# A period's second scale product behind a down projection's first column tile, and the last group of activations scaled two tiles later

## The chip, the cores and the metric

One Trainium2 chip, of which the kernel uses one core. The metric is the device time of one execution in microseconds, the median of three runs. TensorE is called PE here, VectorE DVE, ScalarE ACT, GpSimd POOL and SyncE SP.

## What is computed

The reference is one residual block on an input of 512 tokens by 2048 features: a normalised input goes through a combined projection into a gated linear recurrence and a banded attention, both are projected back and added, and a gated feed-forward follows. The change is in the feed-forward:

```
h2 = rms_norm(x, g_ffn[l])
up = causal_dwconv(h2 @ w_up[l], conv_w[l], conv_b[l])
a, gate = jnp.split(up, 2, axis=-1)
x = x + (a * jax.nn.silu(gate)) @ w_down[l]
```

w_up has 2 x 5632 columns, w_down 5632 rows and 2048 columns; all is float32 at entry and exit.

## The kernel before

The kernel is one program of straight code, and PE sets its pace. The feed-forward has 44 column pairs (`NPAIR_FF`); a pair is 128 columns of a and the 128 columns of gate that belong to them. The first four (`N_LEAD`) are made in `lead`. Each of the pairs 4 to 43 is a **unit** (`up_unit`): a Strassen scheme with seven products instead of eight, each of 8 x 3 small matmuls (`mm3`: high by high, high by low, low by high, in 16 bits). The products read weight tiles that ACT (line 889) and DVE (line 890) split into a high and a low half in `split16`. Behind each unit but the first stand two **downs** (`down`), each a block of w_down with two column tiles of 12 matmuls; DVE adds each column tile to the result (line 1078). One unit with its two downs is a **period**. 88 downs are listed in `DOWNS`; `N_BESIDE` = 78 of them stand beside units, ten follow the last unit.

**The order of the preparation.** `plan_unit` appends to the list `todo`, for each unit, seven steps (`start`, which splits the tile a22, then a11, s1, a11 again after an addition, a12, a12 again, s3), and then one `down_split` for each of its downs. Each step puts one split tile into `ready`. A product or a down begins with `take(3)`:

```
while len(ready) < 1 + n_ahead and todo:
    todo.pop(0)()
return ready.pop(0)
```

so that four tiles are ready before one is taken. Counted from the first step of a unit j with two downs, the steps are 0 to 6 for the products, 7 and 8 for the two downs, and step 9 is the `start` of unit j + 1. Product p takes step p, and steps up to p + 3 have been written by then.

**The scale chain.** Before its first split a period needs its scales. `period_scales(j, ds)` loads the two raw w_down tiles of the period (`down_loads`), has ACT sum the absolute values of each row of the unit's four raw tiles and of the two w_down tiles (`abs_sums`, line 895), and calls `scales`: DVE takes maxima (line 770), ACT writes them on a diagonal, one for the unit and one for the downs (line 771, tile `dg`, a pool with one buffer), PE multiplies the diagonals by ones (line 773, the small product), and DVE makes the scale and its inverse from the result (lines 774 to 776). `start` calls `period_scales` where the unit's dictionary has no "s" yet. `period_scales` also makes the scaled filter taps (lines 930 and 932).

The raw w_down tiles come from the tag "raw" of the pool `wp`, which has three buffers (in the last ten downs every second pair takes "ur" buffers); a split tile has three buffers of each of two tags. The loads of w_down, w_up and the rest are issued by SP (line 876), the accumulating ones by POOL (line 881).

**The activations.** Four units make one group of activations. `m_scale(g)` runs `scales` once over the group and `m_split` splits each of its four tiles (lines 856 and 857). These calls wait in the list `later`, from which each product runs one at its end; behind the last unit (43) the loop over `steps` runs all that are left, at once, before the down that follows it in `steps`. Downs 72 to 79 read group 9, downs 80 to 87 group 10, the group of units 40 to 43.

Program order is the priority with which the framework's scheduler lays the instructions into each engine's queue; the queues themselves run strictly in order.

Of the kernel before, what the change touches and what calls it, by code (L numbers as in the profile page):

```python
# [18 lines left out]
T = 512  # L19
# [4 lines left out]
NPAIR_FF = 44  # L24
# [28 lines left out]
def block_kernel(ctx: ExitStack, tc: tile.TileContext, xT, wst, cols, bias_t, masks, yT):  # L53
# [76 lines left out]
    def mm3(ps, sh, sl, mh, ml, start, stop):  # L130
        PE.matmul(ps, lhsT=sh, rhs=mh, start=start, stop=False)  # L131
        PE.matmul(ps, lhsT=sh, rhs=ml, start=False, stop=False)  # L132
        PE.matmul(ps, lhsT=sl, rhs=mh, start=False, stop=stop)  # L133


    colt = cst.tile([P, NC], F32, name="colt")
# [623 lines left out]

    def scales(sets, bound):


        n = len(sets)
        t = sm_t()
        dg = dgp.tile([P, 2, P], BF16, tag="dg", name=nm("dg"))
        for i, r in enumerate(sets):
            V.tensor_reduce(out=t[:, i:i + 1], in_=r, axis=mybir.AxisListType.X, op=ALU.max)  # L770
            A.activation(dg[:, i], ident, AF.Copy, scale=t[:, i:i + 1])  # L771
        psm = c3(mx_t()[:, 0:2 * P], 2)
        PE.matmul(psm[:, 0:n], lhsT=on1b, rhs=dg[:, 0:n], start=True, stop=True)
        V.tensor_reduce(out=t[:, 2:2 + n], in_=psm[:, 0:n], axis=mybir.AxisListType.X, op=ALU.max)
        V.tensor_scalar(out=t[:, 4:4 + n], in0=t[:, 2:2 + n], scalar1=1.01 / bound, scalar2=1e-30, op0=ALU.mult, op1=ALU.add)
        V.reciprocal(out=t[:, 6:6 + n], in_=t[:, 4:4 + n])
        return [(t[:, 4 + i:5 + i], t[:, 6 + i:7 + i]) for i in range(n)]
# [115 lines left out]
    def abs_sums(r, tiles):  # L893
        for k, t in enumerate(tiles):
            A.activation(junk_t(), t, AF.Abs, accum_out=r[:, k:k + 1])  # L895
# [15 lines left out]
        new = ur_t if at_end >= 0 and at_end % 4 == 0 else raw_t  # L911
        return [load(new(), N_DOWN + 8 * g + c2) for g, c2 in ds]

    def period_scales(j, ds):

        r = sm_t()
        sets = []
        u = units.get(j)
        if u is not None:
            abs_sums(r[:, 0:4], [u[n] for n in ("s1", "a22", "a11", "a12")])  # L920
            sets.append(r[:, 0:4])
        if ds:
            raws = down_loads(ds)
            abs_sums(r[:, 4:8], raws)
            sets.append(r[:, 4:4 + len(ds)])
        sc = scales(sets, BND)
        dt = [(raw, *sc[-1]) for raw in raws] if ds else []
        if u is not None:
            h = cwp.tile([P, 1], F32, tag="uh", name=nm("uh"))
            V.tensor_tensor(out=h, in0=sc[0][0], in1=inv_h, op=ALU.mult)  # L930
            cw = cwp.tile([P, 2, 3], F32, tag="cw", name=nm("cw"))
            A.activation(cw, c3(colt[:, C_CW:C_CW + 3 * 88], 2)[:, :, 3 * j:3 * j + 3], AF.Copy, scale=h)
            u.update(s=sc[0][1], cw=cw, ds=dt)
        return dt

    def plan_unit(j, ds):
        u = units.setdefault(j, {})

        def whl(n):
            ready.append(split16(u[n], u["s"]))  # L940

        def start():
            if "s" not in u:
                period_scales(j, ds)
            whl("a22")

        def s2():
            V.tensor_tensor(out=u["a11"], in0=u["s1"], in1=u["a11"], op=ALU.add)  # L948
            whl("a11")

        def s4():
            V.tensor_tensor(out=u["a12"], in0=u["a11"], in1=u["a12"], op=ALU.add)
            whl("a12")
            if j + 1 < NPAIR_FF:
                unit_loads(j + 1)

        def s3():
            i = N_MIX + 16 + 4 * (j - N_LEAD)
            u["s3"] = load_sum(raw_t() if j == N_LEAD else spare, i, i + 2)
            whl("s3")  # L960

        todo.extend([start, lambda: whl("a11"), lambda: whl("s1"), s2, lambda: whl("a12"), s4, s3])
        todo.extend([lambda k=k: down_split(u["ds"][k]) for k in range(len(ds))])

    def down_split(d):
        raw, inv, s = d
# [2 lines left out]
    def plan_downs(ds):  # L969

        st = []

        def one(k):
            if k == 0:
                st.extend(period_scales(None, ds))
            down_split(st[k])
        todo.extend([lambda k=k: one(k) for k in range(len(ds))])

# [45 lines left out]
    def lead():  # L1024
        half = N_LEAD // 2
        n = 0
        for j in range(half):
            u = c3(ur_t(), 2)
            for e in range(2):
                ps = mm_t()  # L1030
                for h in range(2):
                    wh, wl = next_w()
                    for k in range(8):
                        cs = slice(k * P, (k + 1) * P)
                        kt = 8 * h + k
                        mm3(ps, wh[:, cs], wl[:, cs], hh[kt], hl_[kt], kt == 0, kt == KT - 1)
                        if n == 0 and k == 3:
                            finish_r2()
                    if n in (2, 4, 6):
                        t_prep(n // 2 - 1)  # L1040
                    n += 1
                evict_r2(ps, u[:, e])
            lead_taps(j, [u[:, 0], u[:, 1]], (ssa, rmask)[j])
        unit_loads(N_LEAD)
        pss = [mm_t() for _ in range(2 * half)]
        for i in range(8):
            wh, wl = next_w()
            for e, kt in enumerate((i, i + 8)):
                for c in range(2 * half):
                    cs = slice((4 * e + c) * P, (4 * e + c + 1) * P)  # L1050
                    mm3(pss[c], wh[:, cs], wl[:, cs], hh[kt], hl_[kt], i + e == 0, i + e == 8)
            if i in (1, 2, 4, 6, 7):
                t_prep((0, 3, 4, 0, 5, 0, 6, 7)[i])
            if i == 4:
                period_scales(N_LEAD, [])
        us = [evict_r2(ps, actp.tile([P, T], F32, tag="act", name=nm("u"))) for ps in pss]
        later.extend([lambda j=j: lead_taps(half + j, us[2 * j:2 * j + 2]) for j in range(half)])

    def down(g, c2):
        t, inv_w = take(3)  # L1060
        mg, parts = groups[g]
        inv = cwp.tile([P, 1], F32, tag="inv", name=nm("inv"))
        V.tensor_tensor(out=inv, in0=inv_w, in1=mg[:, 1:2], op=ALU.mult)
        for cc in range(2):
# [5 lines left out]
            for ps, ts_ in zip(pss, cuts):  # L1070
                for k in range(4):
                    cs = slice((cc * 4 + k) * P, (cc * 4 + k + 1) * P)
                    cl = slice(1024 + (cc * 4 + k) * P, 1024 + (cc * 4 + k + 1) * P)
                    m = parts[k]
                    mm3(ps[:, ts_], t[:, cs], t[:, cl], m[:, ts_], m[:, T + ts_.start:T + ts_.stop], k == 0, k == 3)
            eng = nc.gpsimd if c < KT - 3 else nc.sync
            for ps, ts_ in zip(pss, cuts):
                V.scalar_tensor_tensor(out=acc[c][:, ts_], in0=ps[:, ts_], scalar=inv, in1=acc[c][:, ts_], op0=ALU.mult, op1=ALU.add)  # L1078
# [22 lines left out]
    for st in steps:  # L1101
        if isinstance(st, tuple):
            down(*st)
            continue
        up_unit(st)
        if st == N_LEAD:
# [3 lines left out]
        elif st % 4 == 3:  # L1110
            g = st // 4
            later.append(lambda g=g: (m_scale(g), m_split(4 * g)))
            later.extend([lambda j=j: m_split(j) for j in range(4 * g + 1, 4 * g + 4)])
        if st == NPAIR_FF - 1:
            while later:
                later.pop(0)()


def _level_masks(np):
# [121 lines left out]
```

## Time and profile before

| | |
|---|---|
| median of three runs | 2281.39 us (2280.96 to 2282.54) |
| the profiled execution | 2279.07 us, of which the span from the first to the last instruction is 2277.3 us |
| PE busy | 2200.5 us (97% of the span), granted clock 0.996 |
| DVE busy | 1672.4 us (73%) |
| ACT busy | 1336.8 us (59%) |
| moved by DMA | 294.21 MB, mean 129 GB/s |

"Busy" is the time in which an engine executes something, added up over the whole span; "granted clock" is TensorE's clock as a share of full speed. An idle time is named by the instruction that ended it, after the arrow.

### The profile page before, as it was taken

The page shows a single profiled execution, that of the slowest core. Times are in us where ns is not written, and L with a number is a line of the kernel's source. Part 1 is how long each engine was busy: PE and PEld are TensorE (multiplying, and loading weights), DVE is VectorE, ACT ScalarE, POOL GpSimd, SP SyncE. Part 2 cuts the span into 40 slices and gives each one's busy share as a digit, 9 for nine tenths or more (in the row PEclk, how much of TensorE's full clock was granted, in tenths as well). Part 3 has the DMA queues.
Part 4 walks back from the last instruction along what each step waited for, and adds up shares of the span by engine and source line. Part 5 has one row for each costly group of instructions (what it writes and reads, how often), then busy time and mean ns, then how long its engine had stood idle before and what let it go on. Part 6 is the DMA issues. An engine that isn't in the chain of part 4 may idle for free.

```text
span 2277.3 us, 34675 instructions
## 1 busy us (share of the span) xinstructions
PE 2200.5 (97%) x13667; PEld 1694.6 (74%) x13667; DVE 1672.4 (73%) x2729; ACT 1336.8 (59%) x2119; POOL 271.3 (12%) x261
## 2 busy tenths in 40 slices
PE   9999999999999999998999999999999999999989
PEld 7888888788888888785667777776776777777654
DVE  7678658857658744787777777787877777778764
ACT  5455445545445424457676767776667776767661
POOL 5223123310001103100000000000000000000001
PEclk9999999999999999999999999999999999999999
DMA  6222222232222333445555565555555666655532
GB/s 211 88 70 75 84 93 65 77 99 84 86 91 93 125 117 101 129 140 131 166 158 164 161 162 162 158 157 153 148 164 158 167 167 167 158 156 160 149 91 83
DMA packets 82755, 294.21 MB, mean 129 GB/s; under 512 B 9568, under 2 KB 10208, under 8 KB 82592
## 3 DMA queue, kind: packets, MB, share of 16 engines
q1 hardware_dynamic: 68112, 240.34, 32.4%
q0 software_dynamic: 14480, 51.65, 12.0%
q8 instruction: 107, 1.75, 0.3%
q14 instruction: 56, 0.46, 0.1%
HBM read 287.76 MB, written 4.19 MB: 128 GB/s over the span
## 4 chain that ended last, share of the span: by engine, by line
PE 49%; DVE 28%; ACT 11%; issue 6%; DMA 6%; POOL 0%; SPq 0%; ACTq 0%; DVEq 0%; POOLq 0%
PE mm L131 12%; PE mm L133 12%; PE mm L132 12%; DVE whl L890 8%; DMA raw<-wst 5%; ACT junk L895 4%; ACT whl L889 4%; DVE vo L1078 3%; PE mx L133 3%; PE mx L131 3%; PE mx L132 3%; DVE vo L828 2%; DVE vo L829 2%; DVE ur L948 1%; ACT dg L771 1%
## 5 line engine op out<-in xcount | busy, mean ns | idle before, releaser
L131 PE MATMUL mm<-th,whl 128*128 128x256 f16 x2240 | 612.5, 273 | 5.9 <-ACT whl L889 5.9
L133 PE MATMUL mm<-th,whl 128*128 128x256 f16 x2240 | 612.3, 273 | 2.6 <-DVE whl L890 2.6
L132 PE MATMUL mm<-tl,whl 128*128 128x256 f16 x2240 | 612.3, 273 | 0.0
L131 PE MATMUL mm<-act,whi 128*128 128x512 f32 x1024 | 406.4, 397 | 0.0
L133 PE MATMUL mm<-act,wlo 128*128 128x512 f32 x1024 | 399.4, 390 | 0.0
L131 PEld LDWEIGHTS <-whl 128*128 128x128 f16 x2948 | 289.1, 98 | 147.9 <-issue 32.0
L132 PE MATMUL mm<-act,whi 128*128 128x512 f32 x1024 | 398.8, 389 | 0.0
L133 PEld LDWEIGHTS <-whl 128*128 128x128 f16 x2948 | 289.2, 98 | 133.7 <-issue 22.5
L132 PEld LDWEIGHTS <-whl 128*128 128x128 f16 x2948 | 289.2, 98 | 108.5 <-issue 0.8
L889 ACT ACTIVATE whl<-ur,sm 128x1024 f16<-128x1024 f32 x206 | 231.1, 1142 | 154.2 <-DVE ur L948 52.1
L119 ACT CAST whi<-raw 128x1024 fp32r<-128x1024 f32 (+1 forms) x161 | 167.7, 1042 | 228.9 <-PE mm L132 183.7
L890 DVE SCALAR_TENSOR_TENSOR whl<-ur,sm,whl 128x1024 f16<-128x1024 f32 x206 | 261.4, 1277 | 41.0 <-ACT whl L889 41.0
L122 DVE TENSOR_TENSOR wlo<-raw,whi 128x1024 fp32r<-128x1024 f32 (+1 forms) x161 | 209.5, 1302 | 91.5 <-ACT whi L119 86.7
L131 PE MATMUL mx<-mhl,whl 128*128 128x512 f16 x708 | 268.5, 379 | 0.0
L132 PE MATMUL mx<-mhl,whl 128*128 128x512 f16 x708 | 268.4, 379 | 0.0
L133 PE MATMUL mx<-mhl,whl 128*128 128x512 f16 x708 | 268.2, 379 | 0.0
L133 PEld LDWEIGHTS mm<-act,wlo 128*128 128x128 f32 x1024 | 192.2, 188 | 41.2
L131 PEld LDWEIGHTS mm<-act,whi 128*128 128x128 f32 x1024 | 192.4, 188 | 38.8 <-issue 0.5
L132 PEld LDWEIGHTS mm<-act,whi 128*128 128x128 f32 x1024 | 192.5, 188 | 38.1 <-issue 0.5
L895 ACT ACTIVATE junk<-ur 128x1024 f16<-128x1024 f32 x146 | 152.1, 1044 | 0.0
L1078 DVE SCALAR_TENSOR_TENSOR vo<-mx,inv,vo 128x512 f32<-128x512 f32 x177 | 130.3, 741 | 25.1 <-PE mx L133 25.1
L890 DVE SCALAR_TENSOR_TENSOR whl<-raw,sm,whl 128x1024 f16<-128x1024 f32 x83 | 106.3, 1283 | 43.1 <-ACT whl L889 42.2
(285 smaller groups left out, 3022.7 us busy)
## 6 DMA issues: line engine op xcount, KB each, us to landing
raw<-wst SPq DMA_DIRECT2D x242, 512.0 KB, 3.5
ur<-wst SPq DMA_DIRECT2D x146, 512.0 KB, 3.5
spare<-wst SPq DMA_DIRECT2D x59, 512.0 KB, 4.8
ur<-wst POOLq DMA_DIRECT2D x40, 512.0 KB, 5.6
spare<-wst POOLq DMA_DIRECT2D x39, 512.0 KB, 8.0
vo<-xT SPq DMA_DIRECT2D x16, 256.0 KB, 5.3
vo<-xT POOLq DMA_DIRECT2D x16, 256.0 KB, 3.1
yT<-vo POOLq DMA_DIRECT2D x13, 256.0 KB, 2.3
```

Source lines behind the costliest of these rows:

```text
L119: A.copy(out=hi[:, c], in_=raw[:, c])
L122: V.tensor_tensor(out=lo[:, c], in0=raw[:, c], in1=hi[:, c].bitcast(F32), op=ALU.subtract)
L131: PE.matmul(ps, lhsT=sh, rhs=mh, start=start, stop=False)
L132: PE.matmul(ps, lhsT=sh, rhs=ml, start=False, stop=False)
L133: PE.matmul(ps, lhsT=sl, rhs=mh, start=False, stop=stop)
L771: A.activation(dg[:, i], ident, AF.Copy, scale=t[:, i:i + 1])
L828: V.scalar_tensor_tensor(out=y[:, 1:], in0=u[:, :T - 1], scalar=cw[:, 1:2], in1=y[:, 1:], op0=ALU.mult, op1=ALU.add)
L829: V.scalar_tensor_tensor(out=y[:, 2:], in0=u[:, :T - 2], scalar=cw[:, 0:1], in1=y[:, 2:], op0=ALU.mult, op1=ALU.add)
L889: A.activation(t[:, 0:1024], x, AF.Copy, scale=s)
L890: V.scalar_tensor_tensor(out=t[:, 1024:], in0=x, scalar=s, in1=t[:, 0:1024], op0=ALU.mult, op1=ALU.subtract)
L895: A.activation(junk_t(), t, AF.Abs, accum_out=r[:, k:k + 1])
L1078: V.scalar_tensor_tensor(out=acc[c][:, ts_], in0=ps[:, ts_], scalar=inv, in1=acc[c][:, ts_], op0=ALU.mult, op1=ALU.add)
```

## The change

`period_scales` is cut in two: `period_sums(j, ds)` (the loads and the sums of absolute values) and `period_scales(state, after)` (`scales` and what follows). The last `down_split` step of a unit j (step 8), from unit 5 on, now also calls `period_sums` for unit j + 1 and keeps its result in `sums_of`. The first down of a pair takes `take(1)` instead of `take(3)`, and behind the matmuls of its first column tile it calls `period_scales` on the kept result, with the small product ordered behind the last of these matmuls on PE (`issue_after` adds that order). `start` is left as it is, but for the call in it being written with both halves. At the end, the calls in `later` are no longer run right behind unit 43: the first of them (`m_scale` and one `m_split`) follows the down with number 77, the others the down with number 78.

```
-    def scales(sets, bound):
+    def scales(sets, bound, after=None):
...
-        PE.matmul(psm[:, 0:n], lhsT=on1b, rhs=dg[:, 0:n], start=True, stop=True)
+        with tc.issue_after(after.ins) if after is not None else ExitStack():
+            PE.matmul(psm[:, 0:n], lhsT=on1b, rhs=dg[:, 0:n], start=True, stop=True)
...
-    def period_scales(j, ds):
+    def period_sums(j, ds):
 
         r = sm_t()
-        sets = []
         u = units.get(j)
         if u is not None:
             abs_sums(r[:, 0:4], [u[n] for n in ("s1", "a22", "a11", "a12")])
-            sets.append(r[:, 0:4])
-        if ds:
-            raws = down_loads(ds)
-            abs_sums(r[:, 4:8], raws)
-            sets.append(r[:, 4:4 + len(ds)])
-        sc = scales(sets, BND)
-        dt = [(raw, *sc[-1]) for raw in raws] if ds else []
+        raws = down_loads(ds) if ds else []
+        abs_sums(r[:, 4:8], raws)
+        return j, r, raws
+
+    def period_scales(state, after=None):
+
+        j, r, raws = state
+        u = units.get(j)
+        sets = ([r[:, 0:4]] if u is not None else []) + ([r[:, 4:4 + len(raws)]] if raws else [])
+        sc = scales(sets, BND, after)
+        dt = [(raw, *sc[-1]) for raw in raws]
...
         def start():
             if "s" not in u:
-                period_scales(j, ds)
+                period_scales(period_sums(j, ds))
             whl("a22")
...
-        todo.extend([lambda k=k: down_split(u["ds"][k]) for k in range(len(ds))])
+        for k in range(len(ds)):
+            todo.append(lambda k=k: down_split(u["ds"][k]))
+        if ds and j + 1 < NPAIR_FF:
+            def sums(f=todo.pop()):
+                f()
+                sums_of[j + 1] = period_sums(j + 1, DOWNS[2 * (j - N_LEAD):2 * (j - N_LEAD) + 2])
+            todo.append(sums)
...
     def down(g, c2):
-        t, inv_w = take(3)
+        i = DOWNS.index((g, c2))
+        first = i % 2 == 0 and i < N_BESIDE - 2
+        t, inv_w = take(1 if first else 3)
...
-                    mm3(ps[:, ts_], t[:, cs], t[:, cl], m[:, ts_], m[:, T + ts_.start:T + ts_.stop], k == 0, k == 3)
+                    last_mm = mm3(ps[:, ts_], t[:, cs], t[:, cl], m[:, ts_], m[:, T + ts_.start:T + ts_.stop], k == 0, k == 3)
+            if first and cc == 0:
+                j = N_LEAD + 2 + i // 2
+                period_scales(sums_of.pop(j), last_mm)
...
             down(*st)
+            if st in DOWNS[N_BESIDE - 1:N_BESIDE + 1] and later:
+                later.pop(0)()
+                while later and st == DOWNS[N_BESIDE]:
+                    later.pop(0)()
             continue
...
-        if st == NPAIR_FF - 1:
-            while later:
-                later.pop(0)()
```

Two calls that the diff also touches keep their place: `plan_downs` and `lead` call the two halves one inside the other, and `mm3` returns its last matmul.

## Rows read from the trace of the kernel before

**Rows 1.** The page's first part: busy time, share and instructions of each engine.
```profile
PE 2200.5 (97%) x13667; PEld 1694.6 (74%) x13667; DVE 1672.4 (73%) x2729; ACT 1336.8 (59%) x2119; POOL 271.3 (12%) x261
```

**Rows 2.** Waits of PE over the whole span: us in total, times, longest.
```profile
PE mx L773 <- ACT dg L771: 46.8, 34, 9.7
```

**Rows 3.** Waits of PE from 1063 to 2170 us.
```profile
PE mx L773 <- ACT dg L771: 35.2, 31, 2.0
```

**Rows 4.** Stages: length, PE, PEld, DVE, ACT, POOL busy, clock, DMA.
```profile
1511.50:1631.40 119.90, 115.81 (x870) 84.92 (x869) 94.08 (x142) 83.49 (x126) 6.99 (x8) 1.00 0.57 158
...
1030.00:1063.00 33.00, 23.60 (x168) 17.89 (x168) 22.89 (x39) 22.93 (x37) 0.87 (x1) 0.85 0.46 132
1063.00:2170.00 1107.00, 1071.75 (x8042) 786.08 (x8041) 870.22 (x1317) 772.56 (x1159) 65.56 (x75) 1.00 0.59 160
```

**Rows 5.** Timeline of PE, one period: start, us, what.
```profile
1543.75 0.38 PE L131 MATMUL mx<-mhl,whl 128*128 128x512 f16 x1
...
1554.11 0.27 PE L131 MATMUL mm<-th,whl 128*128 128x256 f16 x1
...
1570.64 0.27 PE L773 MATMUL mx<-dg,on1b 128*128 128x256 bf16 x1 [0.65 <-ACT dg L771]
...
1583.73 0.27 PE L131 MATMUL mm<-th,whl 128*128 128x256 f16 x1
```

**Rows 6.** Timeline of ACT, the same period.
```profile
1563.70 1.13 ACT L889 ACTIVATE whl<-raw,sm 128x1024 f16<-128x1024 f32 x1
...
1568.82 1.06 ACT L895 ACTIVATE junk<-raw 128x1024 f16<-128x1024 f32 x1 [0.87 <-DMA raw<-wst]
...
1569.87 0.72 ACT L771 ACTIVATE dg<-ident,sm 128x128 bf16<-128x128 f32 x2
1571.89 1.15 ACT L889 ACTIVATE whl<-ur,sm 128x1024 f16<-128x1024 f32 x1 [1.30 <-DVE inv L1063]
1572.95 0.29 ACT L932 ACTIVATE cw<-colt,uh 128x6 f32<-128x6 f32 x1
```

**Rows 7.** Timeline of DVE, the same period.
```profile
1564.87 1.28 DVE L890 SCALAR_TENSOR_TENSOR whl<-raw,sm,whl 128x1024 f16<-128x1024 f32 x1 [1.83 <-ACT whl L889]
...
1573.07 1.28 DVE L890 SCALAR_TENSOR_TENSOR whl<-ur,sm,whl 128x1024 f16<-128x1024 f32 x1 [1.17 <-ACT whl L889]
```

**Rows 8.** Timeline of SP's issues, the same period.
```profile
1563.06 3.44 SPq L876 DMA_DIRECT2D raw<-wst  x2
```

**Rows 9.** The tile raw from 1150 to 2100 us.
```profile
DMA to landing us min/median/max: 4.7/5.7/9.4
```

**Rows 10.** The tile raw from 2180 to 2230 us.
```profile
DMA to landing us min/median/max: 3.5/3.5/3.6
```

**Rows 11.** The instructions of line 895 in four periods: length, ACT busy.
```profile
1511.50:1631.40 119.90, 25.95 (x48) 1.00 0.57 158
```

**Rows 12.** Groups of ACT's instructions by shape: count, busy, mean ns.
```profile
L856 ACT ACTIVATE mhl<-m,mg 128x512 f16<-128x512 f32 x42 | 27.9, 714 | 5.3 <-DVE mg L850 5.3
```

**Rows 13.** Timeline of PE behind the last unit.
```profile
2198.83 0.27 PE L133 MATMUL mm<-th,whl 128*128 128x256 f16 x1
2208.77 0.27 PE L773 MATMUL mx<-dg,on1b 128*128 128x128 bf16 x1 [9.67 <-ACT dg L771]
2208.83 0.63 PE L131 MATMUL mx<-mhl,whl 128*128 128x512 f16 x1
2209.26 0.63 PE L132 MATMUL mx<-mhl,whl 128*128 128x512 f16 x1
```

**Rows 14.** Stage behind that wait, columns as in rows 4.
```profile
2208.80:2214.00 5.20, 5.20 (x15) 1.96 (x15) 3.62 (x10) 4.02 (x7) 0.00 (x0) 0.55 0.01 3
```

**Rows 15.** Timeline of ACT behind the last unit.
```profile
2190.13 1.14 ACT L889 ACTIVATE whl<-raw,sm 128x1024 f16<-128x1024 f32 x1
...
2209.98 2.56 ACT L856 ACTIVATE mhl<-m,mg 128x512 f16<-128x512 f32 x4 [1.25 <-DVE mg L850]
...
2217.93 2.17 ACT L889 ACTIVATE whl<-raw,sm 128x1024 f16<-128x1024 f32 x2
```

More of the change, by code (lines that the diff above doesn't have):

```diff
@@ L132, in mm3 @@
         PE.matmul(ps, lhsT=sh, rhs=ml, start=False, stop=False)
-        PE.matmul(ps, lhsT=sl, rhs=mh, start=False, stop=stop)
+        return PE.matmul(ps, lhsT=sl, rhs=mh, start=False, stop=stop)
     colt = cst.tile([P, NC], F32, name="colt")
@@ L962, in plan_unit @@
         todo.extend([start, lambda: whl("a11"), lambda: whl("s1"), s2, lambda: whl("a12"), s4, s3])
-        todo.extend([lambda k=k: down_split(u["ds"][k]) for k in range(len(ds))])
+        for k in range(len(ds)):
[5 more added lines that the diff above has]
+            todo.append(sums)
+    sums_of = {}
     def down_split(d):
@@ L974, in one @@
             if k == 0:
-                st.extend(period_scales(None, ds))
+                st.extend(period_scales(period_sums(None, ds)))
             down_split(st[k])
@@ L1054, in lead @@
             if i == 4:
-                period_scales(N_LEAD, [])
+                period_scales(period_sums(N_LEAD, []))
         us = [evict_r2(ps, actp.tile([P, T], F32, tag="act", name=nm("u"))) for ps in pss]
```

## The prediction

> **What bounds the kernel now.** I read the busy times first: PE works 97% of the span, DVE 73%, ACT 59% [rows 1], so a change pays where PE stands still, and costs where it makes PE stand still. Then PE's waits, over the whole span: 46.8 us in 34 waits of the small product (line 773) for the diagonal that ACT writes [rows 2]. They are of two kinds. Between 1063 and 2170 us, the steady part, there are 35.2 us in 31 waits, none over 2.0 us [rows 3], which is 35.2 / 38 = 0.93 us for each of the units 6 to 43 and their periods. One wait alone, behind the last unit, is 9.67 us long [rows 13]. Third, the stages: four periods last 119.90 us, of which PE is busy 115.81, so 28.95 us a period is PE's floor; ACT is busy 83.49, or 20.87 a period, and DVE 94.08, or 23.5 [rows 4]. Last, the timelines of one period, from PE's first product matmul at 1554.11 to the next at 1583.73 us [rows 5], for what the chain does inside it.
>
> There the last sum of ACT begins at 1568.82 and ends by 1569.87, where the diagonals begin; the small product starts at 1570.64, 0.65 us after PE could have run it; the split of a22 follows on ACT at 1571.89 and on DVE from 1573.07 to 1574.35 [rows 5 to 7]. So from the end of the last sum to a finished a22 the chain takes 4.48 us. PE needs a22 only at 1583.73, or 1583.08 without the 0.65 us of waiting. The chain itself is 8.7 us early. PE waits not for its result but because the small product stands too early in PE's in-order queue. To move that product back looks right.
>
> **What the change adds: the work of a period's scales, twice.** The count of steps decides it. Product 5 takes with three ahead and so writes step 8; there the new code runs `period_sums` for unit j + 1. Product 6 still takes with three ahead (the diff leaves it), so it writes step 9, the `start` of unit j + 1. At that point no "s" is there: `period_sums` has not set it, only `period_scales` does, and that is called later, in the first down. So `start` runs both halves anew: it loads the same two w_down tiles again, sums all six tiles again, and issues its own small product, with no order imposed. The first down, after product 6, then runs `period_scales` on the first set of sums, and overwrites the scales. This happens for units 6 to 43, 38 times. `take(1)` in the first down comes one take too late to prevent it. The wait that should go belongs to the chain that stays.
>
> Per period the second set costs:
> - ACT: line 895 fills 25.95 us in four periods with 24 sums, 6.49 a period [rows 11]; two diagonals 0.72 and the taps 0.29 [rows 6]; together 7.5. ACT comes to 28.4 us of PE's 28.95.
> - SP: two more loads of 512 KB each, into the three "raw" buffers.
> - PE: one more small product. The period of rows 5 holds, besides the downs (1543.75 to 1554.11, 10.36 us), 169 matmuls in 29.62 - 10.36 - 0.65 = 18.6 us, 0.11 each; 38 of them are 4 us. The ordered product finds its diagonal ready, since its sums are the first set, and I cost no wait for it; the cover is the first column tile, 12 matmuls of 0.22, 2.6 us, ahead of it, and without that cover it would wait like the present one, up to 2.0 us.
> - DVE: five small instructions, near 1 us; it has 28.95 - 23.5 = 5.4 us idle, so nothing; with no idle time left it would be 38 us.
>
> Two moves are free. `period_sums` is written one product earlier, but its loads stand behind full buffers on SP and go out when these come free, as now; nothing on POOL is passed. `take(1)` leaves the split of a11 to the second down, two takes before its use; if ACT had no such lead, a split of 1.15 us [rows 6] would be late.
>
> **Where it shows: the chain of `start` comes late.** Of the three raw buffers, two hold the first set until the next unit's steps 7 and 8. The second set must pass through the third, one tile after the other. That buffer comes free when the old w_down tile has been split, at 1564.87 + 1.28 = 1566.15 [rows 7], just where SP issues the second of its raw loads now (1563.06 + 3.44 less the issue) [rows 8]. A load then lands 4.7 to 9.4 us later, 5.7 in the median [rows 9], by 1571.9. ACT meanwhile: now its sums end at 1569.87; in the hole of 0.87 us [rows 6] goes one of the four repeated unit sums, the other three follow to 1573.1, and the first repeated w_down tile to 1574.1. Only then can the second load be issued. With L for its landing, and 1.05 us for its sum, a22 is ready at 1574.2 + L + 1.05 + 4.48 = 1579.7 + L, against 1583.08. For L the rows of this stretch give 4.7 as the least and 5.7 as median, for pairs of loads [rows 9]; behind the last unit, with the queue empty, 3.5 [rows 10]. The second load goes alone, but into a stretch with other traffic, so I take 4.7: a22 is 1.3 us late. With 5.7 it is 2.3, with 3.5 about 0.1.
>
> The Trainium skill has another figure: "DMA: Bandwidth & Descriptors", section "Anatomy of one DMA", fits a GpSimd-issued transfer as 2.0 us plus its bytes over 436 GB/s, by which 512 KB would land in an estimated 3.2 us. By that page L + 1579.7 = 1582.9, just in time, and three periods in four would not wait at all. The trace does not agree: 4.7 is the least it shows in this stretch.
>
> One period in four also holds the four `m_split` of a group, 4 x 0.71 = 2.9 us of ACT ahead of the sums [rows 12], and its diagonal; they push the chain by about 3 us more, since ACT then has no hole. So the mean stall is (3 x 1.3 + 4.3) / 4 = 2.05 us in place of 0.93: +1.1 a period, 38 times, **+43 us**. The bounds: L of 3.5 gives (3 x 0.1 + 3.1) / 4 = 0.85, -3 us; L of 5.7 gives 3.05, +81 us.
>
> **The first units.** From 1030 to 1063 us PE is busy 23.60 of 33.00 us, with ACT at 22.93 and the clock at 0.85 [rows 4]: here splits already come late. Two or three doubled chains of 7.5 us fall into it or right behind; between 0 and 22 us, of which I take **8**.
>
> **The end.** Now PE stops at 2198.83 and goes on at 2208.77, and the next matmuls start 0.43 us apart instead of 10.36 / 48 = 0.22 [rows 5, 13]: the granted clock of those 5.20 us is 0.55 [rows 14], near the lower level of 1.2 GHz, after 9.67 us of idleness. 5.2 x 0.45 = 2.3 us go there, 12.0 in all. After the change two downs of group 9, 10.36 us, stand ahead of the small product, and two more ahead of the first use of group 10. Their tiles are split (the last by ACT from 2190.13) [rows 15]. The activations are scaled from 2209.98 as now and split by 2213, before PE needs them at 2199 + 20.7 = 2219.7. What is late next are the w_down tiles of down 80 and 81, split by ACT from 2217.93 to 2220.1 [rows 15], with DVE a good 1 us behind: at worst 2 us late, at best moved forward into ACT's holes, as their sums now stand ahead of `m_scale` in program order. **-11 us**, between -9.5 and -12.
>
> **Sum** against the profiled execution: 2279.1 + 43 + 8 + 4 - 11 = 2323; the median of the runs stood 2.3 above it, so **2325 us**, 1.9% slower. With the short landing and no start-up cost it is 2281.4 - 3 + 4 - 11 = 2271; with the long one and 22 us of start-up 2281.4 + 81 + 22 + 4 - 9.5 = 2379.
>
> **The rivals.**
> - *The doubled chain stays hidden* (ends on the other side). The a22 split is 8.7 us early; the doubling may use that up and no more. It is decided by the order on ACT: if the first repeated w_down tile is summed when it lands (1571.9) and not behind the unit's tiles, or if L is below 4, `start` is in time, PE's waits stay at about 0.9 us, and the end alone counts: 2281.4 + 4 - 11 = 2274, with the last of the present waits gone as well some 35 less, 2240. For it: ACT idles 1107 - 772.56 = 334 us in the 37 periods of the steady part, 9.0 each [rows 4], more than the 7.5 added. Against it: the two loads in series, which no idle engine shortens.
> - *ACT becomes the bound.* 28.4 us of work leave 0.5 us for waits, and ACT waits 9.0 a period now. If, late as it is, a half of these stay, a period takes 32.9 us against 29.9: +3.0 x 38 = 114, less the end: 2281.4 + 114 + 4 - 11 + 8 = 2396. For it: ACT and DVE answer each other in a22, in the addition to a11 and in the taps. Against it: ACT's waits shrink when it runs late.
> - *The change does what it says*, the 35.2 us go and the end too: 2281.4 - 35 - 11 = 2235. It would need `start` to find its scales, which the order of steps excludes, or the chain of `start` to be on time and its product placed late enough.
>
> **How the numbers follow.** A change of under 0.2%, 4.6 us, cannot be told from none. Chances: the forecast, a22 late by 1 to 3 us, 0.50 (its own range 2290 to 2365); ACT the bound, 2365 to 2430, 0.22; the doubling hidden, 2255 to 2287, 0.21, of which 0.07 lies within 0.2%; as it says, 0.07. Faster is 0.14 + 0.07 = 0.21, the same 0.07, slower 0.72. The range leaves out the 0.07 and about half of the ACT case: 2258 to 2390.
>
> **What would show it.** Right: line 895 with 228 activations more, ACT's busy time up by 38 x 7.5 = 285 us, 76 more loads, 40 MB; line 773 with 38 more matmuls, of which the ordered ones do not wait; PE waiting each period either for a22 (lines 131 or 133 for whl) or at the unordered small product; the 9.67 us gone, and no clock below full behind the last unit. The step on L is wrong if the second repeated raw load lands in 3.5 us or is not issued behind the sum of the first. The whole is wrong if the counts of lines 895 and 773 do not rise.

## The result and the profile after

The changed kernel takes 2621.97 us, the median of four runs (2613.67 to 2627.08), against 2281.18 us of the kernel before on the same chip (four runs too, with the three of the table before among them): a ratio of 1.1493, 95% interval [1.1459, 1.1527]. It is 14.9% slower. The forecast was 2325 us with a range of 2258 to 2390: the sign is right, and the size is far off.

The page's first part, after (compare [rows 1]); the span is 2622.5 us against 2277.3:

```profile
PE 2281.1 (87%) x13705; PEld 1716.8 (65%) x13705; DVE 1718.9 (66%) x2957; ACT 1608.4 (61%) x2689; POOL 271.2 (10%) x261
```

PE's idle time went from 2277.3 - 2200.5 = 76.8 us to 2622.5 - 2281.1 = 341.4, by 264.6 us; PE's busy time grew by 80.6. Together these are the 345.2 us of the span. ACT has 272 us more work (forecast 285), and PE 38 matmuls more, as forecast. So the work is doubled as the prediction said. What it costs is another matter.

In the changed file the small product is line 774, the sums line 896, the splits lines 890 and 891. PE's waits over the whole span (compare [rows 2]):

```profile
PE mx L774 <- ACT dg L771: 310.5, 42, 10.5
...
PE mm L131 <- ACT whl L890: 7.2, 4, 4.2
...
PE mm L133 <- DVE whl L891: 2.5, 2, 1.6
```

and from 1063 to 2510 us alone (compare [rows 3]):

```profile
PE mx L774 <- ACT dg L771: 294.1, 37, 10.5
```

In the steady part it is 294.1 / 37 = 7.9 us at each wait, where it was 0.93 a period and the prediction said 2.05. Only the small product waits; the waits for split tiles, where the prediction priced the stall, are 9.7 us in the whole run, against 8.5 before. PE's timeline shows which of the two small products it is (compare [rows 5]):

```profile
1532.75 0.27 PE L133 MATMUL mm<-th,whl 128*128 128x256 f16 x1
1540.70 0.37 PE L774 MATMUL mx<-dg,on1b 128*128 128x256 bf16 x1 [7.67 <-ACT dg L771]
1540.86 0.63 PE L131 MATMUL mx<-mhl,whl 128*128 128x512 f16 x1
1541.29 0.63 PE L132 MATMUL mx<-mhl,whl 128*128 128x512 f16 x1
...
1544.78 0.27 PE L774 MATMUL mx<-dg,on1b 128*128 128x256 bf16 x1
```

The product without an order, that of `start`, now stands behind the unit's last matmul and ahead of both downs; in [rows 5] it stands ahead of the unit's last 24 matmuls (1570.64 us, with the first matmul of the downs at 1573.37). The ordered one, 12 matmuls on, waits for nothing. Behind the wait the downs' matmuls start 0.43 us apart and not 0.22. Windows over the wait, the two downs and the next unit (columns as in [rows 4]):

```profile
1533.10:1540.70 7.60, 0.00 (x1) 0.00 (x1) 4.50 (x10) 4.40 (x8) 0.00 (x0) 0.74 0.19 71
1540.70:1552.60 11.90, 11.90 (x50) 5.27 (x50) 9.14 (x19) 6.58 (x11) 0.87 (x1) 0.88 0.39 100
1552.60:1571.00 18.40, 18.40 (x170) 16.45 (x168) 10.02 (x12) 15.44 (x25) 1.74 (x2) 1.00 0.84 232
```

Behind the idle stretch the first matmuls take twice their time, as at 1.2 GHz, the lower of the two levels; the granted clock of the downs' window is 0.88 on the mean, and it is back at 1.00 in the unit. That is where most of the 80 us of PE's busy time come from: the downs' 700 matmuls of line 131 take 297.9 us in all, against 266.3, and the units' 2240 still take 612.7, against 612.5.

ACT's timeline ahead of that wait (compare [rows 6]): six sums, six more, and both repeated w_down tiles with a wait of their own.

```profile
1521.28 1.04 ACT L896 ACTIVATE junk<-ur 128x1024 f16<-128x1024 f32 x1
...
1527.60 1.06 ACT L896 ACTIVATE junk<-raw 128x1024 f16<-128x1024 f32 x1
...
1531.78 1.04 ACT L896 ACTIVATE junk<-ur 128x1024 f16<-128x1024 f32 x1
...
1534.06 1.06 ACT L896 ACTIVATE junk<-raw 128x1024 f16<-128x1024 f32 x1 [1.15 <-DMA raw<-wst]
...
1538.87 1.06 ACT L896 ACTIVATE junk<-raw 128x1024 f16<-128x1024 f32 x1 [1.96 <-DMA raw<-wst]
...
1540.24 0.40 ACT L771 ACTIVATE dg<-ident,sm 128x128 bf16<-128x128 f32 x1 [0.22 <-DVE sm L770]
...
1543.16 1.13 ACT L890 ACTIVATE whl<-ur,sm 128x1024 f16<-128x1024 f32 x1
1546.92 1.15 ACT L890 ACTIVATE whl<-ur,sm 128x1024 f16<-128x1024 f32 x1 [2.62 <-DVE sm L777]
```

Without the second set the diagonal could have been written at 1528.7; it is written at 1540.24. The last line shows a second thing: the split of a11, behind that of a22, waits 2.62 us for a reciprocal. It is that of the second, ordered chain, which has replaced the scales of the first.

### The profile page after: what moved, and what is told of

It reads as the page before. It is cut to its first block, busy times and chain, and to the rows that moved or that the text cites. A ratio compares the mean times of both kernels' runs of the same rounds, so it can differ in the third digit from the quotient of the medians.

```text
span 2622.5 us, 35767 instructions
## 1 busy us (share of the span) xinstructions
PE 2281.1 (87%) x13705; PEld 1716.8 (65%) x13705; DVE 1718.9 (66%) x2957; ACT 1608.4 (61%) x2689; POOL 271.2 (10%) x261
## 4 chain that ended last, share of the span: by engine, by line
PE 54%; ACT 15%; DMA 15%; DVE 12%; issue 4%; POOL 0%; SPq 0%; ACTq 0%; DVEq 0%; POOLq 0%
DMA raw<-wst 13%; PE mm L131 10%; PE mm L133 10%; PE mm L132 10%; ACT junk L896 9%; PE mx L131 6%; PE mx L132 6%; PE mx L133 6%; DVE whl L891 4%; ACT whl L890 3%; ACT mhl L857 1%; DMA spare<-wst 1%; DVE wlo L122 1%; PE mx L774 1%; DVE wk L216 1%
## 5 line engine op out<-in xcount | busy, mean ns | idle before, releaser
L131 PE MATMUL mm<-th,whl 128*128 128x256 f16 x2240 | 612.7, 274 | 7.2 <-ACT whl L890 7.2
L132 PE MATMUL mm<-tl,whl 128*128 128x256 f16 x2240 | 612.5, 273 | 0.0
L131 PEld LDWEIGHTS <-whl 128*128 128x128 f16 x2948 | 294.8, 100 | 451.2 <-issue 347.8
L133 PEld LDWEIGHTS <-whl 128*128 128x128 f16 x2948 | 295.2, 100 | 134.0 <-issue 35.3
L132 PEld LDWEIGHTS <-whl 128*128 128x128 f16 x2948 | 296.1, 100 | 121.8 <-issue 27.1
L131 PE MATMUL mx<-mhl,whl 128*128 128x512 f16 x708 | 300.1, 424 | 0.0
L774 PE MATMUL mx<-dg,on1b 128*128 128x256 bf16 (+1 forms) x95 | 29.5, 310 | 310.5 <-ACT dg L771 310.5
L132 PE MATMUL mx<-mhl,whl 128*128 128x512 f16 x708 | 297.0, 419 | 0.0
L133 PE MATMUL mx<-mhl,whl 128*128 128x512 f16 x708 | 293.9, 415 | 0.0
L896 ACT ACTIVATE junk<-ur 128x1024 f16<-128x1024 f32 x279 | 290.5, 1043 | 0.0
L896 ACT ACTIVATE junk<-raw 128x1024 f16<-128x1024 f32 x158 | 165.9, 1051 | 95.8 <-DMA raw<-wst 95.1
L133 PEld LDWEIGHTS mm<-act,wlo 128*128 128x128 f32 x1024 | 192.2, 188 | 41.2
```

The source lines that it names most:

```text
L133: return PE.matmul(ps, lhsT=sl, rhs=mh, start=False, stop=stop)
```

## The experiments

Each was compared with the kernel before on its own chip (medians of 2279 to 2283 us).

**Without the doubling.** `once`: the changed kernel, in which the last product of units 5 to 42 takes with two ahead, so that `start` comes after `period_scales`.

```diff
-    def product(ps, b):
-        t = take(3)
+    def product(ps, b, n=3):
+        t = take(n)
...
-        product(bank[2][:, H:], T3)
+        product(bank[2][:, H:], T3, 2 if N_LEAD < j < NPAIR_FF - 1 else 3)
```

> The changed kernel with take(2) in the last product of a unit, so that start comes after the first down and finds its scales: every sum and every small product once. Theory A (the work done twice makes start's diagonal 8 us late, and its small product, ahead of both downs in PE's queue, holds PE for it): the 38 waits of about 8 us go, with them those of before (35 us), and the end gains 11: about 2235 us. Rival B (the product ordered behind the first column tile, or the summing one product earlier, is itself what costs): stays above 2500 us.

Measured: 2345.56 us, ratio 1.027 [1.025, 1.0289]. Nothing is doubled, and still it is 2.7% slower. The expectation failed, and the time lies far below the rival's too. The place behind the first column tile is itself a bad one, or the look-ahead that was given up for it. PE's waits:

```profile
PE mx L774 <- ACT dg L771: 55.3, 40, 5.7
PE mm L133 <- DVE whl L891: 32.7, 56, 1.6
PE mm L131 <- ACT whl L890: 14.1, 10, 3.3
```

Against the kernel before, the waits at the small product grew by 8.5 us, those for split tiles by 38.3 (from 8.5 to 46.8), and PE's busy time by 26.5 (from 2200.5 to 2227.0).

`once_early` asks whether the look-ahead that `once` gave up is the cause.

```diff
                 period_scales(sums_of.pop(j), last_mm)
+                while len(ready) < 3 and todo:
+                    todo.pop(0)()
```

> The kernel 'once' (nothing doubled, the single small product ordered behind the first column tile of the first down), but the steps that take(1) and take(2) held back, the split of a22 among them, are written right behind the scales in the middle of the first down, instead of at the second down. If 'once' lost its 64 us because its look-ahead came down to two tiles and a22's split was written too late, this one recovers them: 2250 to 2285 us, and the matmuls' waits for whl (47 us in 'once') go below 15. If the place itself is too late, because VectorE's evictions and additions of the first column tile stand ahead of the scale chain, the waits for whl stay and it ends at 2320 to 2350 us.

Measured: 2349.46 us, ratio 1.0283 [1.0253, 1.0312]. The look-ahead is not it. What is left is the place. PE's small product and DVE's timeline in this kernel:

```profile
1535.44 0.27 PE L774 MATMUL mx<-dg,on1b 128*128 128x256 bf16 x1 [1.30 <-ACT dg L771]
...
1537.10 0.42 DVE L775 TENSOR_REDUCE sm<-mx 128x2 f32<-128x256 f32 x1
1537.43 0.74 DVE L830 SCALAR_TENSOR_TENSOR vo<-z,cw,vo 128x510 f32<-128x510 f32 x1
1538.09 0.74 DVE L829 SCALAR_TENSOR_TENSOR vo<-z,cw,vo 128x511 f32<-128x511 f32 x1
1538.75 0.16 DVE L776 TENSOR_SCALAR sm<-sm 128x2 f32<-128x2 f32 x1
1538.82 0.74 DVE L1097 SCALAR_TENSOR_TENSOR vo<-mx,inv,vo 128x512 f32<-128x512 f32 x1
1539.48 0.74 DVE L830 SCALAR_TENSOR_TENSOR vo<-z,cw,vo 128x510 f32<-128x510 f32 x1
1540.14 0.15 DVE L777 RECIPROCAL sm<-sm 128x2 f32<-128x2 f32 x1
```

During a down DVE's queue holds the conv taps of the unit just done (lines 829 and 830) and the downs' additions (line 1097), and they stand between the chain's three short steps. From the product to the scales it takes 1540.29 - 1535.44 = 4.85 us, and a22 is split only behind that. No run took these instructions out of DVE's queue; that they are what costs is read from this timeline and from `p6end` below.

**The end alone.** `tail`: the kernel before with nothing but the move of the end.

```diff
             down(*st)
+            if st in DOWNS[N_BESIDE - 1:N_BESIDE + 1] and later:
+                later.pop(0)()
+                while later and st == DOWNS[N_BESIDE]:
+                    later.pop(0)()
             continue
...
-        if st == NPAIR_FF - 1:
-            while later:
-                later.pop(0)()
```

> The kernel before with the move of the last group's scaling alone. Theory: 9.67 us of wait and 2.3 us of slow clock go, up to 2 us come back as a late split behind them: 2270 us, 0.5% faster. Rival: a split or a scale product of the last ten downs is late in its place, and the end gains under 6 us.

Measured: 2281.1 us, ratio 0.9993 [0.998, 1.0007]. The 11 us don't come. PE's small products behind the last unit (compare [rows 13]):

```profile
2209.84 0.27 PE L773 MATMUL mx<-dg,on1b 128*128 128x128 bf16 x1 [5.69 <-ACT dg L771]
2217.00 0.22 PE L773 MATMUL mx<-dg,on1b 128*128 128x128 bf16 x1
2224.78 0.22 PE L773 MATMUL mx<-dg,on1b 128*128 128x128 bf16 x1 [2.38 <-ACT dg L771]
```

The product of `m_scale` at 2217.00 waits no more. The product of the downs 80 and 81 now stands ahead of it and waits 5.69 us, that of the next two downs another 2.38. That is 8.1 us in place of 9.67. The end of the changed kernel is no better: behind 2516 us PE waits 14.5 us in three times, of which 6.4 belong to the last period.

**One set of sums fewer at a time.** `noreload` is the changed kernel, where the second set sums the tiles of the first again, without loading them again.

```diff
-    def period_sums(j, ds):
+    def period_sums(j, ds, raws=None):
...
-        raws = down_loads(ds) if ds else []
+        if raws is None:
+            raws = down_loads(ds) if ds else []
...
-                period_scales(period_sums(j, ds))
+                period_scales(period_sums(j, ds, sums_of[j][2] if j in sums_of else None))
```

> The changed kernel, but start sums the w_down tiles that the first call has loaded instead of loading them again; ACT still sums everything twice, 7.5 us a period more than before. Theory A: the two loads in series go from the chain; the diagonal is then late by ACT's extra work alone, near 3.5 us at the boundary between unit and downs, instead of 8: about 2370 us, 2340 to 2420. Rival C (ACT with 28.4 us of work a period is the bound, whatever is loaded): 2580 us or more. Rival D (the loads alone do it): below 2290.

Measured: 2519.87 us, ratio 1.1036 [1.1018, 1.1055], in none of the ranges expected. The loads in series are 2621.97 - 2519.87 = 102 us of the loss, not most of it; 239 remain without them. The small product still waits 192.2 us in 37 times between 1063 and 2400 us, 5.2 each, where 3.5 were expected.

`noresum` leaves out the second set of sums as well; only `scales` and what follows it are still done twice.

```diff
-                period_scales(period_sums(j, ds))
+                period_scales(sums_of[j] if j in sums_of else period_sums(j, ds))
```

> The changed kernel, in which start takes the sums of step 8 instead of summing and loading again; only the scale chain (two diagonals, small product, five small instructions of VectorE) is still done twice, and the end is as changed. Theory A, the doubled sums and the serial loads are the whole loss, and the unordered small product of start is late only because they are: the sums are then those of the kernel before and stand one product earlier in the order, so start's product waits 1 to 2 us a period as before; the small product's second execution costs 38 x 0.1 = 4 us and ACT 1.0 us a period. About 2285 us, 2275 to 2300. Theory B, a second chain with a product ordered behind the first column tile costs by itself (the scales overwritten, splits and scales waiting for each other): 2330 us or more, with new waits of the downs' matmuls for whl or of the ordered product.

Measured: 2408.57 us, ratio 1.0561 [1.0545, 1.0577]. The repeated sums are 111 us, but theory A falls: a second chain of some ten short instructions costs over 120.

`start_once` has the same sums, one product earlier, and no second chain:

```diff
-                period_scales(period_sums(j, ds))
+                period_scales(sums_of.pop(j) if j in sums_of else period_sums(j, ds))
...
-            if first and cc == 0:
-                j = N_LEAD + 2 + i // 2
-                period_scales(sums_of.pop(j), last_mm)
```

> The sums in step 8 as in the change, but start takes them over and issues the one small product itself, where it stood before; no scales in the first down; the end as changed; look-ahead of three but for the take(1). Theory F (once lost 62 us by the later place of the chain, behind the first column tile, with scales that come late for a22): 2275 to 2285 us, as before. Rival G (the summing one product earlier delays ACT's splits): 2310 or more.

Measured: 2280.13 us, ratio 1.0001 [0.9988, 1.0013]: to write the sums earlier, `take(1)` and the end together cost and give nothing. ACT's diagonals and splits around the chain in `start_once`:

```profile
1513.02 0.72 ACT L771 ACTIVATE dg<-ident,sm 128x128 bf16<-128x128 f32 x2
...
1515.02 1.15 ACT L890 ACTIVATE whl<-ur,sm 128x1024 f16<-128x1024 f32 x1 [1.28 <-DVE uh L934]
...
1516.27 2.17 ACT L890 ACTIVATE whl<-ur,sm 128x1024 f16<-128x1024 f32 x2
```

and in `noresum`:

```profile
1526.47 0.72 ACT L771 ACTIVATE dg<-ident,sm 128x128 bf16<-128x128 f32 x2
...
1527.55 0.69 ACT L771 ACTIVATE dg<-ident,sm 128x128 bf16<-128x128 f32 x2 [0.36 <-PE mx L774]
1528.41 1.15 ACT L890 ACTIVATE whl<-ur,sm 128x1024 f16<-128x1024 f32 x1 [0.17 <-DVE sm L777]
...
1537.69 1.13 ACT L890 ACTIVATE whl<-ur,sm 128x1024 f16<-128x1024 f32 x1
```

The split behind that of a22 comes 1.25 us after it in the one and 9.28 us after it in the other. The second chain writes new scales, and every split from a11 on reads those.

`nouse` is the test of this: `noresum`, with the second chain still computed in full and its results left unused.

```diff
-            u.update(s=sc[0][1], cw=cw, ds=dt)
+            if use:
+                u.update(s=sc[0][1], cw=cw, ds=dt)
...
-                period_scales(sums_of.pop(j), last_mm)
+                period_scales(sums_of.pop(j), last_mm, False)
```

> 'noresum' (sums once, scale chain twice, 2408.6 us), in which the second chain is computed in full, small product, reduction, reciprocal and taps, but its results are left unused: all splits of the unit and of the two downs read the scales of start. Theory A, the 128 us that the second chain costs over 'start_once' come from the splits that must wait for its scales: a11 and all behind it are split only when the reduction behind the first down's first column tile has passed VectorE's queue, so the w_down splits, the loads that wait for their buffers and the next period's last sum come late. Then this kernel gives nearly all back: 2280 to 2305 us. Theory B, the chain's own work and its places in the queues of ACT, VectorE and PE cost it: it stays at 2390 to 2410 us.

Measured: 2301.1 us, ratio 1.0099 [1.0079, 1.0118], within A's figures. 107 of the 128 us come from splits that wait for scales which were already there once; 21 are the chain's own work and places. The 107 us show on PE as shorter waits at the small product (58.2 us in 42 times, against 129.6 in 45 in `noresum`) and as 39.6 us less of busy time. The expectation's path from late splits over late loads to a late sum fits: ACT's sums wait 15.2 us for raw loads between 1100 and 2100 us, against 50.1 in `noresum`; no run tested that path by itself. `noreload_nouse` makes the same edit in `noreload`.

> 'noreload' (sums twice, chain twice, 2519.9 us) with the second chain's results left unused in the same way. If the repeated sums, 6.5 us of ACT ahead of start's product, cost their 111 us whatever the second chain does: 2281 + 111 = 2390, 2370 to 2410 us. If they cost only because the second chain has already made the period's splits late, and would be hidden in ACT's idle time without it: 2290 to 2340 us. If the second chain's overwriting costs nothing: 2520 again.

Measured: 2463.34 us, ratio 1.0818 [1.0792, 1.0844], between the ranges expected. The repeated sums are not hidden without the other loss. They cost 2463.34 - 2301.1 = 162 us by themselves and 111 beside it, so the two losses overlap in part, and no single figure belongs to either.

**The same doubling in the kernel before.** `dup_before` calls `period_scales` twice in `start` and is the kernel before otherwise.

```diff
                 period_scales(j, ds)
+                if j > N_LEAD + 1:
+                    period_scales(j, ds)
```

> The kernel before, with start computing each period's scales twice (loads, sums, small product), and nothing else of the change. Theory A (the doubled work, waited for at small products ahead of the downs, is the whole loss): 2560 to 2650 us, waits of 6 to 9 us a period at the small products. Rival E (the change's other parts, less look-ahead and the summing in step 8, carry a good part of it): below 2480.

Measured: 2532.34 us, ratio 1.1092 [1.1068, 1.1116], a little under the range expected. So doubling costs 250 us with nothing moved. In the change it is 341. The difference was not taken apart; in `dup_before` both chains run ahead of the first split, so no split waits for scales that are written anew in the downs, and no set is held across a unit.

**The order itself.** `nopin` takes only the order off the ordered product.

```diff
-                period_scales(sums_of.pop(j), last_mm)
+                period_scales(sums_of.pop(j))
```

> The changed kernel without the order on the second small product (no issue_after); the double work stays. Theory A: the ordered product never waited, so 2600 to 2640 us as the changed kernel. Rival B (the ordering holds PE or pushes start's product to its place): below 2500 us.

Measured: 2629.51 us, ratio 1.1517 [1.1493, 1.154], the changed kernel's time to within 0.3%. The order that gave the change its name does nothing for the time here, since the ordered product already stands behind that column tile by its place in the program: in `nopin` too it runs 12 matmuls behind the other.

`dup_late` meant to keep the doubling and move `start`'s product behind the first down.

```diff
-            if "s" not in u:
-                period_scales(period_sums(j, ds))
+            if "s" not in u or j > N_LEAD + 1:
+                period_scales(period_sums(j, ds), seen.get("mm"))
...
+            seen["mm"] = last_mm
             if first and cc == 0:
```

> The work stays doubled, but take(2) in a unit's last product moves start with its second small product behind the first down, so PE has 5.2 us of matmuls ahead of the place where it waits. Theory A (it is the place of the product in PE's queue that turns the late chain into a wait): the wait falls by about those 5 us a period; 2345 (the same kernel without the doubling) plus 0 to 100: 2345 to 2450 us. Rival C (ACT's work of 28.4 us a period is the bound wherever PE waits): 2550 us or more.

Measured: 2700.5 us, ratio 1.1836 [1.1814, 1.1858], far from theory A's range. It lies in rival C's, but ACT is busy 1598.3 us of 2698.5, 59%, so ACT's work is not the bound here. The later place in the program moved the repeated sums back in ACT's queue too, behind the taps, so the product's waits rose to 362.2 us in 42 instead of falling. The run does not separate the place of the product from that of its sums, and decides nothing on the place.

**A better place.** `p6end` is the kernel before, with the small product ordered behind the last matmul of the unit's seventh product; the step is written right there.

```diff
-        PE.matmul(psm[:, 0:n], lhsT=on1b, rhs=dg[:, 0:n], start=True, stop=True)
+        with tc.issue_after(pin[0].ins) if pin else ExitStack():
+            PE.matmul(psm[:, 0:n], lhsT=on1b, rhs=dg[:, 0:n], start=True, stop=True)
...
+        pin.append(mm)
+        while len(ready) < 3 and todo:
+            todo.pop(0)()
+        pin.clear()
...
-        product(bank[2][:, H:], T3)
+        product(bank[2][:, H:], T3, 2)
```

> The kernel before, with the small product of start ordered behind the last matmul of the unit's last product instead of ahead of its 24 matmuls (the step runs right behind these matmuls; sums, loads and look-ahead as before). Theory F (the chain is up to 2.0 us late at the old place, and 2.6 us of matmuls now stand ahead): the 35 us of steady waits go, a22 is still 6 us early: 2246 us, 1.5% faster. Rival: the later place delays the scales' chain on DVE, and PE waits for splits instead: 2275 or more.

Measured: 2251.76 us, ratio 0.9869 [0.9852, 0.9885]: 1.3% faster than before. The small product of this kernel and DVE's timeline:

```profile
1500.15 0.27 PE L776 MATMUL mx<-dg,on1b 128*128 128x256 bf16 x1 [0.46 <-ACT dg L773]
...
1500.46 0.42 DVE L777 TENSOR_REDUCE sm<-mx 128x2 f32<-128x256 f32 x1
1500.80 0.68 DVE L1013 TENSOR_TENSOR z<-mm,z 128x512 f32<-128x512 f32 x1
1501.40 0.16 DVE L778 TENSOR_SCALAR sm<-sm 128x2 f32<-128x2 f32 x1
1501.46 0.41 DVE L1014 TENSOR_TENSOR z<-mm,z 128x256 f32<-128x256 f32 x1
1501.80 0.15 DVE L779 RECIPROCAL sm<-sm 128x2 f32<-128x2 f32 x1
```

From the product to the scales it is 1501.95 - 1500.15 = 1.8 us, where it was 4.85 behind the first column tile: only two evictions of the unit stand between, and the taps begin later. Between 1063 and 2150 us PE waits at the small product 8.1 us in 18 times, against the 35.2 in 31 of [rows 3].

`p6end_tail` adds the end's move to it, as the diff of `tail` shows it.

> The kernel 'p6end' (small product ordered behind the last matmul of the unit's last product, 2251.8 us) with the change's move of the end added. If the move of the end is worth nothing, because the wait is handed to the next pair's small product, as in 'tail': 2250 us, 2248 to 2253. If it adds its 10 us: 2241.

Measured: 2250.81 us, ratio 0.9867 [0.9852, 0.9882]: nothing gained, as in `tail`. `best` orders the products of the last downs in the same way, each behind the last matmul of a down.

```diff
+        end = DOWNS.index((g, c2)) >= N_BESIDE - 2
-        t, inv_w = take(3)
+        t, inv_w = take(2 if end else 3)
...
+            if end and cc == 1:
+                pin.append(mm)
+                while len(ready) < 3 and todo:
+                    todo.pop(0)()
+                pin.clear()
```

> 'p6end' with the end moved, and the last pairs of downs treated as the units are: their small product ordered behind the last matmul of the down ahead of it. If the end's wait is a matter of place in PE's queue as the units' was, the 8.1 us that 'tail' still waited go: 2238 to 2245 us. If the diagonal of those pairs is late for another reason (their loads or ACT's queue), the wait moves to the next matmul, for whl: 2248 to 2253 us.

Measured: 2242.24 us, ratio 0.9827 [0.9812, 0.9842], the fastest of all, 1.7% under the kernel before. PE's waits over its whole span (compare [rows 2]):

```profile
PE mx L776 <- ACT dg L773: 13.3, 23, 2.2
```

Behind 2150 us these waits are 2.7 us in two times, against 9.5 in two in `p6end_tail`. So the end did have some 9 us to give (2250.81 - 2242.24), and they hung on the place of the last pairs' products in PE's queue, not on that of `m_scale` alone.

## Why the prediction was wrong

**The doubling: right.** `start` finds no scales and does the whole period again, 38 times: ACT +272 us against 285, 40 MB more, 76 raw loads more. Without it (`start_once`) the loss is gone.

**The chain's timing: nearly right.** The second repeated w_down tile goes alone behind the sum of the first. Forecast was a sum that ends 1574.2 + 4.7 + 1.05 us, with the unit's end at 1583.73 - 10.36 = 1573.4, so 6.6 us behind it; measured, the sum that begins at 1538.87 ends 6.9 us behind the unit's last matmul, which ends at 1533.0. The load is issued behind the sum of the first, as forecast, at 1535.23, and its landing was even shorter than the 4.7 us chosen: the second sum begins 1538.87 - 1535.12 = 3.75 us after the end of the first.

**The step that failed: the price of the lateness.** The prediction charged it at the first use of a22 in the next unit, two downs later: "a22 is 1.3 us late". Among the signs it did name a wait "at the unordered small product", but no term of its sum prices one. `start`'s small product stands ahead of both downs in PE's queue, which runs in order: no matmul and no weight load of the downs ran in the 7.67 us. The cover of 10.36 us, which the downs were to give, is behind the waiting instruction and covers nothing. Charged there, the prediction's own figures give a diagonal at 1574.2 + 4.7 + 1.05 = 1579.95 and the product 0.77 us on [rows 5, 6], at 1580.7, against 1573.4: a wait of 7.3 us, and the period shown has 7.67. (The place behind the unit's last matmul is read from the trace after; at the place of [rows 5], where PE could have run the product from 1569.99 on, the same diagonal gives 10.7.) In the steady part that is 38 x (7.3 - 0.93) = 242 us before the groups' own work, where the prediction had 43. And a22 was never late: its split begins on ACT at 1543.16 and ends on DVE at 1545.6, and the next unit begins at 1552.66. The prediction had itself said that PE waits "because the small product stands too early", and it then asked only whether the ordered product of the pair would wait.

**A term that was missing: the second set of scales.** The prediction notes that the second chain "overwrites the scales" and charges nothing for it. `nouse` shows 107 us for it without the repeated sums and loads, and `noreload_nouse` 57 beside the repeated sums. Neither is to be added to the 242: these runs divide the same loss by what is left out, the 242 by where PE waits. What it costs beside the repeated loads as well, as in the change itself, was not tried. In the changed kernel ACT waits for these scales (line 777) 86.0 us in 33 times between 1100 and 2400 us.

**A second one: the clock.** The prediction used the lower clock for the end alone. Behind the wait shown the first matmuls of the down started 0.43 us apart in place of 0.22, and the downs' matmuls of line 131 take 426 ns in the mean of the run in place of 380; PE's busy time grew by 80.6 us, of which the 38 small products are an estimated 4 (0.11 each).

**The small terms.** For the first units 8 us were taken; up to 1063 us PE's waits for split tiles grew from 8.5 to 9.7, and those at the small product stayed at 1.9, so it was near 1. The present wait of 0.93 us a period divides by 38 what lies in the 37 periods of [rows 3]; it is 0.95, which changes nothing.

**The end: wrong.** -11 us were taken; `tail` measured none. The prediction named the w_down tiles of the downs 80 and 81 as what is late next, "at worst 2 us", again at their use and not at their small product, which waits 5.69 us.

**The rivals.** That ACT becomes the bound (2396 us) lies nearest in time, but ACT is busy 861.63 of 1200 us, 72%, between 1200 and 2400 us. It is late for one instruction, not full. That the change does what it says would not have come true either without the doubling: `once` is 2.7% slower than before. `p6end` shows that of the 35 us of [rows 3] 28 were to be had (2280.13 - 2251.76), with a place just behind the unit.

What the runs add up to, from `start_once`: the second chain's own work 21 us, the splits that wait for its scales 107, the repeated sums 111, the repeated loads in series 102; 2280 + 341 = 2621. That they add up is no test, since each is the difference of two runs of one chain. Taken in another order the shares differ (the sums alone 162). How the 102 us divide between the landings and the one free buffer was not tried.

## What to carry to other kernels

A late result is charged at the first instruction in an in-order queue that waits for it, however small, and work behind that instruction is no cover. When values are computed a second time, look for everything written afterwards that reads the second copy: it waits for the later chain even where the values are the same. A small product belongs where its input has just become ready and the queue of the engine that reads its result is still short: here that was right behind the unit's last matmul (1.3% faster), and not 12 matmuls later in the downs, where the taps and the additions stand in DVE's queue.

## What was not expected of the hardware

Pauses of PE of 7 us, one in each period, cost more than their length: the granted clock was 0.74 in the pause and 0.88 in the window of the downs behind it, whose first matmuls started 0.43 us apart, against 0.22 in a period with a wait of 0.65 us. Over the run that is some 77 us on top of 265 us of added idle time. It is not a fixed share of the idle time: in `noreload`, whose idle time grew by 161 us only, PE's busy time still grew by some 71. By both runs it is an estimated 2 us for each of the 38 pauses, whether of 7.9 us or of 5.2 in the mean.
